# Eight heads' values in one pass: products of 512 columns instead of 256 in a two-layer encoder

## The chip, the cores and the metric

The kernel runs on one core of a Trainium2 chip. The metric is device time in microseconds (us) of one execution, inputs in device memory to output in device memory. TensorE (PE) multiplies matrices into PSUM, which has eight banks of 128 x 512 float32. ACT (ScalarE), DVE (VectorE) and POOL (GpSimd) do the elementwise work, SP (SyncE) issues most transfers.

## The reference, cut to what matters

Two layers over 512 tokens of width 1024; the change is in the first one, neighbourhood attention with 16 heads of 64. Tokens are a grid 64 wide with 8 rows; each query sees a window of all 8 rows and 16 columns, with a learned bias per head.

```python
def mixer_na(xn, w_in, rpb, w_out):
    q, k, v, z = jnp.split(xn @ w_in, 4, axis=-1)      # each (1, 512, 1024)
    o = neighbourhood_attention(q, k, v, rpb)          # 16 heads of 64
    return (o * jax.nn.silu(z)) @ w_out

for i in range(2):
    xn = rmsnorm(x, norm_g[i])
    y = mixer_na(...) if i == 0 else mixer_mla(...)
    h = x + y
    gate = jax.nn.sigmoid(rmsnorm(h, ple_norm[i]) @ ple_w_gate[i])
    x = h + gate * (p[i] @ ple_w_proj[i])
return rmsnorm(x, final_norm)
```

The part of interest is `v = xn @ w_in[:, 2048:3072]`, for all 512 tokens and 16 heads.

## The kernel before, in words

**Precision.** Each operand of a large product is kept as two float32r parts, a high part (a rounded copy, made by ACT) and the rest (made by DVE or POOL). A product then takes three terms: high x high, low x high, high x low. In names, `xh`, `xl` are the two parts of the normalised input turned to columns; `whi`, `wlo` those of a weight.

**Loading weights.** `load_w` (L68) takes 128 x 1024 elements, 512 KB: a transfer from SP into `wraw`, a copy to `whi` on ACT (L78), a subtraction to `wlo` on POOL (L79). Each of the three tiles has three buffers, which all weights of this stage share in turn.

**The first layer's heads.** `na_heads` (L213) goes over eight pairs of heads. `project(j)` makes what pair j needs: for even j first the values of the four heads of pairs j and j+1, then the queries (`sa`, `sb`, 24 products of 512 columns, two copies on ACT, two subtractions on DVE) and the keys (`da`, `db`, `la`, `lb`, likewise, four copies and two subtractions). Values are made token tile by token tile: for each of four tiles `kt` of 128 tokens, 24 products with 128 tokens of `xh` or `xl` held in TensorE and 256 weight columns streamed, over eight k and three terms, the terms one after the other. So every tile wants both loads of its group (`na_v`, 128 x 4 x 256 each) at once. The result goes from bank `mm` to a tile `vt` of 128 x 512, where `v_split` (L204) lays each head's high part and rest side by side (one copy on ACT, L89, one subtraction on DVE, L91). There are eight buffers `vt`, two groups of four heads.

`attend(j)` runs `na_head` (L296) for both heads of the pair: 8 score products of 256 columns (bank `S`, L318 and L319), maximum and exponential on DVE and ACT (L325 to L337), scaling on POOL (L341), 7 transposes of 128 x 128 (bank `T`, L352 and L354), a split on ACT and DVE, and 8 output products with the values held (bank `O`, L366). `combine` adds the halves, `gated` multiplies by the gate where it is ready. Three of the eight gates are made after the last pair (`z_phase`), and the output projection (`out_proj`, L380) follows.

**PSUM.** The eight banks have tags: `mm` two, `S` two, `T` three, `O` one (L63).

**What sets the order.** The code is written as a sequence, `project(j + 1)` ahead of `attend(j)`. The frame it is written in simulates the timeline and plans each engine's order from it, so that instructions of later steps come forward where their operands and buffers are there; the planned order of each engine is then fixed. Buffers of one tag go round in the order in which the code asks for them. A `tile_pool` is memory for a stage; the next stage's tiles lie where the last one's were, and wait tile by tile.

Of the kernel before, what the change touches and what calls it, by code (L numbers as in the profile page):

```python
# [14 lines left out]
F32R = mybir.dt.float32r  # L15
# [4 lines left out]
P = 128  # L20
S = 512
D = 1024
NT = S // P
KD = D // P
# [9 lines left out]
def win(t, r0, r1, off, dims):  # L34

    b = t[r0:r1]
    return bass.AP(tensor=b.tensor, offset=b.offset + off, ap=[list(b.ap[0])] + [list(d) for d in dims])


class Trunk:  # L40
# [99 lines left out]
    def terms(w, xT, ks):  # L140
        whi, wlo = w
        xh, xl = xT
        W = lambda a, k: a[:, k * P:(k + 1) * P]
        X = lambda a, k: a[k // 4][:, k % 4, :]
        t = [(W(whi, k), X(xh, k)) for k in ks]
        t += [(W(whi, k), X(xl, k)) for k in ks]
        t += [(W(wlo, k), X(xh, k)) for k in ks]
        return t
# [64 lines left out]
    def na_heads(self, pool, xT, zs, oT):  # L213
        nc, a = self.nc, self.a
        xh, xl = xT
        X = lambda t, k, kt: t[k // 4][:, k % 4, kt * P:(kt + 1) * P]
        V, A, U = {}, {}, {}

        def project(j):
            if j % 2 == 0:  # L220
                g = j // 2
                wv = [self.load_w(a["na_v"][g, c], 1024) for c in range(2)]
                vts = V[g] = []
                for kt in range(4):
                    ps = self.psum("mm")
                    W = lambda s, k: wv[k // 4][s][:, (k % 4) * 256:(k % 4 + 1) * 256]
                    t = [(X(xh, k, kt), W(0, k)) for k in range(KD)]
                    t += [(X(xl, k, kt), W(0, k)) for k in range(KD)]
                    t += [(X(xh, k, kt), W(1, k)) for k in range(KD)]
                    self.mms(ps[:, :256], t)  # L230
                    vt = pool.tile([P, S], F32R, name="vt", tag="vt", bufs=8)
                    self.v_split(vt, ps[:, :256])
                    vts.append(vt)
            wq = self.load_w(a["na_qk"][j], 1024)
            psq = self.psum("mm")
            self.proj_T(psq, wq, xT)
            sa = pool.tile([P, S], F32R, name="sa", tag="qs", bufs=4)
            sb = pool.tile([P, S], F32R, name="sb", tag="qs", bufs=4)
            nc.scalar.activation(sa[0:64], psq[0:64], AF.Copy, scale=0.125)
            nc.scalar.activation(sb[64:128], psq[64:128], AF.Copy, scale=0.125)  # L240
            nc.vector.scalar_tensor_tensor(sa[64:128], psq[0:64], 0.125, sa[0:64].bitcast(F32),
                                           op0=ALU.mult, op1=ALU.subtract)
            nc.vector.scalar_tensor_tensor(sb[0:64], psq[64:128], 0.125, sb[64:128].bitcast(F32),
                                           op0=ALU.mult, op1=ALU.subtract)
            s0 = []
            for s in (sa, sb):
                e0 = pool.tile([P, P], F32R, name="s0", tag="s0", bufs=4)
                nc.vector.tensor_copy(e0.rearrange("p (a b) -> p a b", a=2),
                                      win(s, 0, P, 0, [[448, 2], [1, 64]]).bitcast(F32))
                s0.append(e0)  # L250
            wk = self.load_w(a["na_qk"][8 + j], 1024)
            psk = self.psum("mm")
            last = self.proj_T(psk, wk, xT)
            da = pool.tile([P, S], F32R, name="da", tag="kd", bufs=4)
            db = pool.tile([P, S], F32R, name="db", tag="kd", bufs=4)
            la, lb = self.rest_k[j % 2]
            nc.scalar.activation(da[0:64], psk[0:64], AF.Copy)
            nc.scalar.activation(da[64:128], psk[0:64], AF.Copy)
            nc.scalar.activation(db[64:128], psk[64:128], AF.Copy)
            nc.scalar.activation(db[0:64], psk[64:128], AF.Copy)  # L260
            nc.vector.tensor_tensor(out=la[0:64], in0=psk[0:64], in1=da[0:64].bitcast(F32), op=ALU.subtract)
            nc.vector.tensor_tensor(out=lb[64:128], in0=psk[64:128], in1=db[64:128].bitcast(F32), op=ALU.subtract)
            A[j] = (sa, sb), s0, (da, db), (la, lb)
            return last

        def attend(j):
            sq, s0, dk, kl = A.pop(j)
            O = []
            for e in range(2):
                c = (2 * j + e) % 4 * P  # L270
                O.append(self.na_head(pool, 2 * j + e, sq[e], s0[e], dk[e], kl[e],
                                      [vt[:, c:c + P] for vt in V[j // 2]]))
            U[j] = self.combine(pool, O[0], O[1], 2 + NLATE)
            if j in zs:
                self.gated(U[j], zs[j], oT, j)


        self.rest_k = []
        for i in range(2):
            la = pool.tile([P, S], F32R, name=f"la{i}", bufs=1)  # L280
            lb = pool.tile([P, S], F32R, name=f"lb{i}", bufs=1)
            nc.gpsimd.memset(la[64:128].bitcast(F32), 0.0)
            nc.gpsimd.memset(lb[0:64].bitcast(F32), 0.0)
            self.rest_k.append((la, lb))
        last = project(0)
        for j in range(8):
            if j < 7:
                last = project(j + 1)
            attend(j)
        late = range(8 - NLATE, 8)  # L290
        zs.update(self.z_phase(a["na_z"], xT, late, self.last_exp.ins))
        for j in late:
            self.gated(U[j], zs[j], oT, j)
        return last.ins
# [594 lines left out]
def layouts(i):  # L889
# [3 lines left out]
    c = np.ascontiguousarray  # L893
    f = {}
# [9 lines left out]
    def tiles(w, n):  # L904
        k, m = w.shape
        return w.reshape(k // P, P, m // n, n).transpose(2, 1, 0, 3)

    w = i["na_w_in"][0]
    f["na_qk"] = c(tiles(w[:, :2048], P).reshape(16, P, 1024))
    f["na_z"] = c(tiles(w[:, 3072:], P).reshape(8, P, 1024))  # L910
    f["na_v"] = c(tiles(w[:, 2048:3072], 256).reshape(4, P, 2, 1024).transpose(0, 2, 1, 3))

    def rows(w):
        return c(tiles(w, S).reshape(2, P, 4, 1024).transpose(0, 2, 1, 3))

    f["na_o"] = rows(i["na_w_out"][0])
    f["mla_o"] = rows(i["mla_w_out"][0])
    f["gate"] = c(np.stack([rows(i["ple_w_gate"][l]) for l in range(2)]))
    f["proj"] = c(np.stack([tiles(i["ple_w_proj"][l], S).reshape(2, P, 1024) for l in range(2)]))
    w = i["mla_w_in"][0]  # L920
# [3 lines left out]
    w = i["mla_w_qb"][0].reshape(384, H, 96)  # L924
# [4 lines left out]
    w = i["mla_w_kvb"][0].reshape(256, H, 128)  # L929
# [49 lines left out]
```

## Time and profile before

| | |
|---|---|
| Three runs, median | 672.58 us (672.41 to 675.2) |
| Profiled execution | 671.05 us, of it span 668.9 us from the first to the last instruction |
| Granted TensorE clock | 0.998 |
| TensorE, busy | 659.1 us, 99% of the span, 3559 products |
| ACT, DVE, POOL, busy | 407.9, 368.4, 394.3 us (61%, 55%, 59%) |
| Loads of the value weights | 8 of 512 KB |
| Value products of this layer | 384 of 128 x 256, starting from 44.7 to 56.9, 80.7 to 97.6, 124.6 to 139.1 and 166.9 to 183.5 us |

A row of the timeline gives the start in us, the length of the row's instructions together, the engine, the line of the code, what is written and read, the shape and the count; in brackets the idle time ahead of it and who ended it. Successive products overlap, so that the price of one is the distance between starts. A row of a window gives the busy time and the count of each engine in a stretch of the span. A row of groups gives a count, the busy time, the mean length in ns, and the idle time ahead.

### The profile page before, as it was taken

To read this page: it belongs to the slowest core of one execution; us is meant where nothing else is said; L and a number is where in the kernel's file an instruction comes from. 1 tells how busy PE (TensorE), PEld (TensorE's weight loads), DVE (VectorE), ACT (ScalarE), POOL (GpSimd) and SP (SyncE) were. 2 spreads that over 40 slices of the span, in tenths; PEclk is the share of its full clock that TensorE was granted. 3 is DMA by queue.
4 is the path that set the end of the run, shared out by engine and by line. 5 is a ranking of instruction groups with operands and counts; after the bars stand their busy time and mean duration, and the time that the engine had idled before them with its cause. 6 is when DMAs were issued, how large, how long until landed. Compare 5 with 4: busy or idle time off the path is not lost.

```text
span 668.9 us, 10166 instructions
## 1 busy us (share of the span) xinstructions
PE 659.1 (99%) x3559; PEld 565.8 (85%) x3559; DVE 368.4 (55%) x828; ACT 407.9 (61%) x813; POOL 394.3 (59%) x322
## 2 busy tenths in 40 slices
PE   9999999999999999999999999999999999999995
PEld 6888898988988888888899887888888888888885
DVE  7461554747746613453624613888888875145434
ACT  7753766657757652653444635887989887436423
POOL 0395546666576565853044526786959786758411
PEclk9999999999999999999999999999999999999999
DMA  9934213222223128534133334120111222664022
GB/s 320 344 121 147 99 53 138 88 86 96 68 99 116 60 98 299 182 110 137 73 116 112 104 102 140 58 75 16 57 49 63 64 97 96 238 247 157 33 79 94
DMA packets 32530, 79.11 MB, mean 118 GB/s; under 512 B 4192, under 2 KB 9056, under 8 KB 32480
## 3 DMA queue, kind: packets, MB, share of 16 engines
q1 hardware_dynamic: 32048, 77.94, 33.9%
q8 instruction: 28, 0.46, 0.3%
q10 hardware_dynamic: 432, 0.52, 0.2%
q14 instruction: 22, 0.18, 0.1%
HBM read 66.92 MB, written 8.39 MB: 113 GB/s over the span
## 4 chain that ended last, share of the span: by engine, by line
PE 92%; POOL 2%; DVE 2%; ACT 1%; DMA 1%; issue 1%; POOLq 0%; SPq 0%; DVEq 0%; ACTq 0%
PE ps_mm L102 50%; PE ps_S L102 12%; PE ps_mm L533 6%; PE ps_T L128 6%; PE ps_O L644 4%; PE ps_T L102 3%; PE ps_O L102 3%; PE ps_O L366 2%; PE ps_mm L173 2%; PE ps_T L354 1%; PE ps_S L319 1%; PE ps_S L318 1%; POOL ex L629 1%; DMA wraw<-proj 1%; DMA qe<-rl 1%
## 5 line engine op out<-in xcount | busy, mean ns | idle before, releaser
L79 POOL TENSOR_TENSOR wlo<-wraw,whi 128x1024 fp32r<-128x1024 f32 (+5 forms) x107 | 209.8, 1978 | 100.3 <-ACT whi L78 79.3
L78 ACT ACTIVATE whi<-wraw 128x1024 fp32r<-128x1024 f32 (+5 forms) x108 | 93.2, 886 | 66.5 <-issue 18.0
L629 POOL TENSOR_TENSOR ex<-ex,rc 128x512 f32<-128x512 f32 x64 | 65.9, 1038 | 25.5 <-DVE rc L628 16.6
L102 PE MATMUL ps_mm<-whi,hnT 128*128 128x512 f32 (+1 forms) x272 | 70.2, 378 | 0.0
L102 PEld LDWEIGHTS ps_mm<-whi,hnT 128*128 128x128 f32 x272 | 49.3, 188 | 9.2
L341 POOL TENSOR_TENSOR ex<-ex,rc 128x128 f32<-128x128 f32 (+1 forms) x64 | 34.3, 560 | 38.0 <-DVE rc L337 36.4
L627 ACT ACTIVATE ex<-ps_S,mx 128x512 f32<-128x512 f32 x64 | 44.0, 688 | 12.3 <-DVE mx L625 11.1
L625 DVE TENSOR_REDUCE mx<-ps_S 128x1 f32<-128x512 f32 x64 | 43.7, 683 | 8.5 <-PE ps_S L102 7.5
L91 DVE TENSOR_TENSOR pt_lo<-ps_T,pt_hi 128x512 fp32r<-128x512 f32 x64 | 43.2, 682 | 7.7 <-ACT pt_hi L89 7.3
L336 ACT ACTIVATE ex<-ex,mx 128x128 f32<-128x128 f32 (+1 forms) x64 | 30.2, 473 | 21.8 <-DVE mx L332 21.4
L102 PE MATMUL ps_mm<-xh,whi 128*128 128x512 f32 x152 | 41.0, 400 | 0.1
L102 PE MATMUL ps_mm<-wlo,hnT 128*128 128x512 f32 (+1 forms) x136 | 40.6, 378 | 0.0
L89 ACT ACTIVATE pt_hi<-ps_T 128x512 fp32r<-128x512 f32 x64 | 37.7, 595 | 4.0 <-PE ps_T L128 3.8
L102 PE MATMUL ps_mm<-xh,wlo 128*128 128x512 f32 x152 | 39.2, 392 | 0.0
L102 PE MATMUL ps_mm<-xl,whi 128*128 128x512 f32 x152 | 38.8, 392 | 0.0
L128 PE MATMUL ps_T<-ident,ex 128*128 128x128 f32 x256 | 38.4, 272 | 0.0
L128 PEld LDWEIGHTS ps_T<-ident,ex 128*128 128x128 f32 x256 | 31.5, 140 | 7.7 <-POOL ex L629 0.4
L194 DVE TENSOR_TENSOR u<-ps_O,u 64x512 f32<-64x512 f32 x32 | 21.9, 686 | 23.1 <-ACT u L193 22.6
L112 POOL TENSOR_TENSOR rs<-ss,half 128x1 f32<-128x1 f32 x20 | 12.7, 638 | 35.0 <-DVE ss L111 34.9
L102 PEld LDWEIGHTS ps_mm<-xl,whi 128*128 128x128 f32 x152 | 28.1, 188 | 5.8
L102 PEld LDWEIGHTS ps_mm<-xh,wlo 128*128 128x128 f32 x152 | 28.1, 188 | 5.5
L463 DVE TENSOR_TENSOR sg<-pe,sg 128x512 f32<-128x512 f32 (+1 forms) x17 | 12.4, 728 | 34.4 <-ACT sg L462 34.4
(342 smaller groups left out, 1668.5 us busy)
## 6 DMA issues: line engine op xcount, KB each, us to landing
pe<-pe SPq DMA_DIRECT2D x32, 256.0 KB, 3.2
wraw<-na_qk SPq DMA_DIRECT2D x16, 512.0 KB, 3.2
wraw<-gate SPq DMA_DIRECT2D x16, 512.0 KB, 3.2
wraw<-na_v SPq DMA_DIRECT2D x8, 512.0 KB, 3.3
wraw<-na_o SPq DMA_DIRECT2D x8, 512.0 KB, 3.4
wraw<-mla_z SPq DMA_DIRECT2D x8, 512.0 KB, 3.5
wraw<-mla_o SPq DMA_DIRECT2D x8, 512.0 KB, 3.3
wraw<-na_z SPq DMA_DIRECT2D x6, 512.0 KB, 5.5
```

The source lines that it names most:

```text
L78: nc.scalar.activation(hi[:, c], raw[:, c], AF.Copy)
L79: f = lambda e, c=c: e.tensor_tensor(out=lo[:, c], in0=raw[:, c], in1=hi[:, c].bitcast(F32), op=ALU.subtract)
L89: self.last_copy = nc.scalar.activation(hi, src, AF.Copy, scale=scale)
L91: nc.vector.tensor_tensor(out=lo, in0=src, in1=hi.bitcast(F32), op=ALU.subtract)
L102: last = self.last_mm = nc.tensor.matmul(out, l, r, start=i == 0, stop=i == n - 1)
L128: self.last_mm = self.nc.tensor.transpose(t[:, i * P:(i + 1) * P], b, self.ident)
L336: self.last_exp = nc.scalar.activation(e, e, AF.Exp, bias=mx[:, qt:qt + 1], accum_out=sm[:, qt:qt + 1])
L341: nc.gpsimd.tensor_tensor(out=e, in0=e, in1=rc[:, qt:qt + 1].to_broadcast([P, e.shape[1]]), op=ALU.mult)
L533: self.last_mm = nc.tensor.matmul(PS[key], *terms[i], start=i == 0, stop=i == len(terms) - 1)
L625: nc.vector.reduce_max(mx, sp, axis=AX.X, negate=True)
L627: nc.scalar.activation(ex, sp, AF.Exp, bias=mx, accum_out=sm)
L629: nc.gpsimd.tensor_tensor(out=ex, in0=ex, in1=rc.to_broadcast([P, S]), op=ALU.mult)
```

## The change

Values are made for eight heads at once (two groups in place of four), in products of 512 columns, chunk by chunk: for each of four loads (`na_v` has the new layout 128 x 2 x 512, two k to a load) all token tiles of the call get their 6 products, so a call keeps one bank open per token tile. The first group is made ahead of everything else, for four token tiles in banks T, T, T and O. The second is made in two bouts of two token tiles each in both banks `mm`, ahead of `attend(1)` and `attend(2)`; each bout loads the whole second group. A finished bank is copied out by two calls of `v_split`, each to a tile `vt` for four heads, as before. There are twelve buffers `vt` instead of eight; the second bout's tiles take the buffers of heads 0 to 3. Values no longer stand in `project`.

```diff
+        def values(g, kts, banks):
+
+            pss = [self.psum(b) for b in banks]
+            for c in range(4):
+                w = self.load_w(a["na_v"][g, c], 1024)
+                for i, (s, r) in enumerate(((0, 0), (1, 0), (0, 1))):
+                    for kt, ps in zip(kts, pss):
+                        for k in (2 * c, 2 * c + 1):
+                            nc.tensor.matmul(ps, X((xh, xl)[s], k, kt), w[r][:, k % 2 * S:(k % 2 + 1) * S],
+                                             start=k == 0 and i == 0, stop=k == KD - 1 and i == 2)
+            for e in range(2):
+                for kt in kts:
+                    V[2 * g + e, kt] = pool.tile([P, S], F32R, name="vt", tag="vt", bufs=12)
+            for kt, ps in zip(kts, pss):
+                for e in range(2):
+                    self.v_split(V[2 * g + e, kt], ps[:, e * 256:(e + 1) * 256])
+
         def project(j):
-            if j % 2 == 0:
-                g = j // 2
-                wv = [self.load_w(a["na_v"][g, c], 1024) for c in range(2)]
-                vts = V[g] = []
-                for kt in range(4):
-                    ps = self.psum("mm")
-                    W = lambda s, k: wv[k // 4][s][:, (k % 4) * 256:(k % 4 + 1) * 256]
-                    t = [(X(xh, k, kt), W(0, k)) for k in range(KD)]
-                    t += [(X(xl, k, kt), W(0, k)) for k in range(KD)]
-                    t += [(X(xh, k, kt), W(1, k)) for k in range(KD)]
-                    self.mms(ps[:, :256], t)
-                    vt = pool.tile([P, S], F32R, name="vt", tag="vt", bufs=8)
-                    self.v_split(vt, ps[:, :256])
-                    vts.append(vt)
             wq = self.load_w(a["na_qk"][j], 1024)
...
-                                      [vt[:, c:c + P] for vt in V[j // 2]]))
+                                      [V[j // 2, kt][:, c:c + P] for kt in range(4)]))
...
+        values(0, range(4), ("T", "T", "T", "O"))
         last = project(0)
         for j in range(8):
             if j < 7:
                 last = project(j + 1)
+            if j in (1, 2):
+                values(1, (2 * j - 2, 2 * j - 1), ("mm", "mm"))
             attend(j)
...
-    f["na_v"] = c(tiles(w[:, 2048:3072], 256).reshape(4, P, 2, 1024).transpose(0, 2, 1, 3))
...
+    f["na_v"] = rows(w[:, 2048:3072])
```

## The prediction

> **What bounds the kernel now.** I read the page first: busy times and the chain that ended last.
>
> ```profile
> span 668.9 us, 10166 instructions
> PE 659.1 (99%) x3559; PEld 565.8 (85%) x3559; DVE 368.4 (55%) x828; ACT 407.9 (61%) x813; POOL 394.3 (59%) x322
> PE 92%; POOL 2%; DVE 2%; ACT 1%; DMA 1%; issue 1%; POOLq 0%; SPq 0%; DVEq 0%; ACTq 0%
> PE ps_mm L102 50%; PE ps_S L102 12%; PE ps_mm L533 6%; PE ps_T L128 6%; PE ps_O L644 4%; PE ps_T L102 3%; PE ps_O L102 3%; PE ps_O L366 2%; PE ps_mm L173 2%; PE ps_T L354 1%; PE ps_S L319 1%; PE ps_S L318 1%; POOL ex L629 1%; DMA wraw<-proj 1%; DMA qe<-rl 1%
> ```
>
> TensorE is busy all the time and makes 92% of the chain; the others stand near 60%. So a product removed counts in full, and work on other engines counts only where TensorE comes to wait. Then the windows, over the stage of the first layer's heads that the change touches:
>
> ```profile
> 45.00:57.00 12.00, 11.48 (x96) 11.28 (x95) 1.90 (x4) 3.17 (x7) 7.18 (x7) 1.00 0.43 138
> 80.00:103.00 23.00, 23.00 (x176) 22.08 (x175) 13.08 (x48) 15.72 (x39) 13.84 (x16) 1.00 0.15 48
> 225.00:243.00 18.00, 17.92 (x102) 15.20 (x101) 9.41 (x24) 12.19 (x24) 10.81 (x11) 1.00 0.09 30
> ```
> ```profile
> 57.00:243.00 186.00, 185.92 (x1131) 165.17 (x1130) 105.92 (x332) 122.79 (x273) 113.90 (x104) 1.00 0.26 88
> ```
>
> Columns: length, then busy time and count of PE, PEld, DVE, ACT, POOL, granted clock (1.00), DMA share, GB/s. From 57 to 243 us TensorE idles 0.08 us of 186; only the first values (45 to 57) lose 0.5. There is almost no idle time to win, so the price of one product decides. It is read from the timeline of TensorE by the distance of starts (the durations overlap):
>
> ```profile
> 46.64 0.64 PE L102 MATMUL ps_mm<-wlo,xh 128*128 128x256 f32 x4
> 47.80 0.74 PE L102 MATMUL ps_mm<-wlo,xh 128*128 128x256 f32 x4 [0.52 <-POOL wlo L79]
> 48.38 1.12 PE L102 MATMUL ps_mm<-whi,xh 128*128 128x256 f32 x8
> ...
> 57.02 2.00 PE L102 MATMUL ps_mm<-xh,whi 128*128 128x512 f32 x8
> ...
> 67.92 1.98 PE L102 MATMUL ps_mm<-xh,whi 128*128 128x512 f32 x8
> ```
>
> **The products.** From 48.38 to 57.02 lie three token tiles of 24 products of 256 columns: 8.64/72 = 0.1200 us each. From 57.02 to 67.92 lie 48 products of 512 columns: 10.90/48 = 0.2271 us. Now the values take 4 groups x 4 tiles x 24 = 384 narrow products, 46.08 us. Afterwards it is 2 x 4 x 24 = 192 wide ones, 43.60 us. The columns are the same; two narrow products cost 12.9 ns more than one wide one. Term 1: -2.48 us.
>
> The Trainium skill, TensorE: Matmul & The Clock Gate, section Back-to-back issue gap, gives a warm distance of N/2.4 + 2.5 ns. By it two narrow products cost only 2.5 ns more than a wide one, term 1 would be an estimated -0.48 us, and the time below would end 2.0 us higher. The rows differ from it (120.0 where it gives 109.2, 227.1 where it gives 215.8), so they decide.
>
> **The wait for the low half.** The first group runs all eight k of the high weights, then wants the low half of the second load. From 46.64, eight products take 48.38 - 46.64 = 1.74 us where 8 x 0.1200 = 0.96 would do: 0.78 us lost. Why it is late:
>
> ```profile
> 42.40 3.00 POOL L796 TENSOR_TENSOR xl<-xT,xh 128x512 fp32r<-128x512 f32 x2
> 45.35 4.75 POOL L79 TENSOR_TENSOR wlo<-wraw,whi 128x1024 fp32r<-128x1024 f32 x2
> ```
> ```profile
> 44.16 1.05 ACT L78 ACTIVATE whi<-wraw 128x1024 fp32r<-128x1024 f32 x1
> ```
>
> POOL is in xl until 45.35; the second low half is ready at 47.7. The new order goes load by load: a load of two k feeds 24 wide products, 5.45 us, and the low half is wanted by the last eight only. If the first wide product starts at 44.7, load 2's low half is wanted at 44.7 + 5.45 + 3.63 = 53.8, 6 us after it is there. The third load takes the slot that the first query weights have now (high half at 44.16, low done at 50.1; wanted at 55.6 and 59.3). The fourth reuses the first load's buffer, free at 50.2: 1.05 + 2.4 us bring it to 53.7, wanted at 61. The two loads put ahead of the queries delay those on SP, but they are wanted only at 66.5. Term 2: -0.78 us, between that and 0.
>
> **Loads and copies.** Each bout loads the whole second group, so 12 loads replace 8. Their prices, and those of the copies:
>
> ```profile
> L78 ACT ACTIVATE whi<-wraw 128x1024 fp32r<-128x1024 f32 x26 | 27.2, 1055 | 23.2 <-issue 17.8 <-PE ps_mm L102 2.4 <-POOL wlo L79 2.0
> L89 ACT ACTIVATE vt<-ps_mm 128x256 fp32r<-128x256 f32 x13 | 4.8, 371 | 1.3 <-PE ps_mm L102 1.3
> ```
> ```profile
> L91 DVE TENSOR_TENSOR vt<-ps_mm,vt 128x256 fp32r<-128x256 f32 x13 | 5.5, 420 | 6.0 <-ACT vt L89 5.7
> ```
> ```profile
> L79 POOL TENSOR_TENSOR wlo<-wraw,whi 128x1024 fp32r<-128x1024 f32 x26 | 62.2, 2397 | 27.5 <-ACT whi L78 15.8 <-PE ps_mm L102 6.0 <-ACT ph L89 2.9
> ```
> ```profile
> wraw<-na_v SPq DMA_DIRECT2D x8, 512.0 KB, 3.3
> ```
>
> ACT gains 4 x 1.055 = 4.2 us, POOL 4 x 2.397 = 9.6 us, SP four issues, the DMA engines 2.1 MB at a share of 0.26. The 16 copies keep their shape. Per pair of heads outside a bout, from the 57 to 243 row: ACT (122.79 - 27.4 - 4.8)/8 + 2 x 1.055 = 13.4 us, DVE (105.92 - 5.5)/8 = 12.6, POOL (113.90 - 62.2)/8 + 2 x 2.397 = 11.3. TensorE's own time for a pair is 48 x 0.2271 = 10.9 plus 46 attention products, at most 0.12 each, 5.5: 16.4 us. A pair with a bout has 27.3 us on TensorE, against ACT 13.4 + 4.2 + 1.5 = 19.1 and POOL 11.3 + 9.6 = 20.9. Inside the bout alone a load feeds 12 products, 2.73 us, where POOL needs 2.40: it holds if POOL does little else then, or attention products stretch the bout. All of it hidden on average; the cover is TensorE's 27 us, and without it up to four low halves would show, 9.6 us.
>
> **The handover of banks.** The bout fills both mm banks at once. Until now four tiles went through them in turn, and the bank of the keys had time to be emptied:
>
> ```profile
> 77.97 1.98 PE L102 MATMUL ps_mm<-xh,wlo 128*128 128x512 f32 x8
> 80.63 0.59 ACT L257 ACTIVATE da<-ps_mm 64x512 fp32r<-64x512 f32 x1
> 80.73 0.89 PE L102 MATMUL ps_mm<-whi,xh 128*128 128x256 f32 x6
> 84.17 0.69 DVE L262 TENSOR_TENSOR lb<-ps_mm,db 64x512 fp32r<-64x512 f32 x1
> 85.33 1.12 PE L102 MATMUL ps_mm<-whi,xh 128*128 128x256 f32 x8
> ```
>
> The keys end at 79.95, their bank is free at 84.86: 4.9 us, bridged by the first value tile and attention products. A bout in written order asks for that bank after two products, 0.45 us. At its end the next queries wait for two copies of the first bank, about 2 x 0.371 + 0.420 = 1.2 us. Two bouts at 4.5 + 1.2 us are 11.4 us if nothing bridges them, 0 if all does. But the planner reorders TensorE by readiness:
>
> ```profile
> 229.48 0.62 PE L102 MATMUL ps_S<-whi,oh 128*128 128x512 f32 x2
> ...
> 242.88 0.61 PE L102 MATMUL ps_mm<-whi,oh 128*128 128x512 f32 x2
> ```
>
> Here the output projection's third tile (bank S) runs 13 us before its first (mm), though the code writes the first one first. With three weight buffers it can run three chunks of the bout's first tile ahead, 18 products or 4.1 us. I stand near the bridged end: one wait like the one shown, 0.52, so term 3: +0.5 us.
>
> **The later pairs.** Values leave the later stretches, so heads 8 to 13 have 16.4 us of TensorE per pair as cover. The fastest pace of before, head 12 to head 14:
>
> ```profile
> 203.23 0.28 PE L318 MATMUL ps_S<-da,s 128*128 128x256 f32 x1
> ...
> 216.26 0.28 PE L318 MATMUL ps_S<-da,s 128*128 128x256 f32 x1
> ```
> ```profile
> 73.53 0.23 PE ps_S L318 x2
> ```
>
> 13.0 us for that pair, under 16.4, though part of it beside less projecting; from head 0 (the last row, of the chain) to head 14 it was 142.7 us, 20.4 a pair, in a stage that had more other work. ACT would be at 13.4/16.4 = 82% there. Bounds: 0, or 2 us for each of four pairs, 8. I take another 0.5 us, near the lower end since pace and loads leave room. Term 4: +0.5. The value buffers: the second bout writes into those of heads 0 to 3, whose readers end a project and a bout earlier; nothing. The output stage's tiles move 8 KB up in memory and may wait for the last reader of the values:
>
> ```profile
> 246.00 1.93 SPq L809 DMA_DIRECT2D r<-x  x4
> ```
>
> It does so already, and chunk 4 of the output projection needs the last heads anyway: nothing, at worst one load's 1.05 + 2.4 = 3.5 us.
>
> **Sum.** -2.48 - 0.78 + 0.5 + 0.5 = -2.26 us. The profiled execution took 671.05 us (span 668.9 and 2.15 around it) and would take 668.8. The median shown is 672.58, 1.5 higher; against it I say 670.3 us, -0.34%. About 0.5%, 3.4 us, is what a measurement here can tell from no change, so this is within it.
>
> **Rivals.** Handover: at the start of each bout TensorE stands, because the planner keeps the written order of the two tiles. Against it the reordering at 229 us; for it that the attention pieces that could fill in are short (8 products, 1 us). At the full 11.4 us the time is 672.58 - 3.26 + 11.4 + 0.5 = 681.2, at half of it 675.5; it turns slower by 0.5% from 6.1 us of standing on.
> Late pairs: heads 8 to 13 can't keep 16.4 us per pair, ACT's queue at 82% being served in order. At 2 us a pair the time is 672.58 - 3.26 + 0.5 + 8 = 677.8; the point is 1.5 us a pair. For it the 20.4 us over the whole stage, against it the 13.0 us pair.
> No narrow-product cost: the 12.9 ns belong to the runs at 48 to 57 us, and wide products in the bouts, alternating between two banks, lose them again. Then 672.58 - 0.78 + 1.0 = 672.8. The page's -0.48 lies near it (672.3), its formula being the rule named above. Against it: both distances hold evenly in neighbouring stretches.
>
> **How the numbers follow.** Forecast 0.50: half of it below 669.2, where nothing is given back (669.3) and the runs' scatter (672.41 to 672.58, the profiled one 671.05) adds; half above. Handover 0.22, of it 0.10 slower. Late pairs 0.16, of it 0.12 slower. No narrow cost 0.12, all within. Faster 0.25, same 0.53, slower 0.22. Range: below, 669.3 less 1 us for scatter, 668.3; above, to 677, just short of the late pairs' 677.8, which leaves out both rivals' upper parts, under 2 in 10 with the low end. The forecast alone: 668.3 to 672.
>
> **What would show it.** Term 1: 192 value products of 128x512 at 0.227 us, none of 128x256 on xh or xl. Term 2: no TensorE wait for wlo in the values' first 22 us. Term 3: TensorE's idle time in the two bouts, under 1 us; waits on DVE lb or vt copies would speak for the handover. Term 4: starts of even heads' first score products 16 to 17 us apart with TensorE full. I am wrong if TensorE idles over 2 us between 45 and 245, or if a wide value product costs over 0.235 us.

## The result, and the profile after

The changed kernel takes 680.53 us (median of 4 runs, 679.05 to 680.75), the kernel before 672.5 (671.36 to 675.2): ratio 1.0117, 95% interval 1.0097 to 1.0137. I had said 670.3 us and a range up to 677. The page of the changed kernel, its span, TensorE and the chain:

```profile
span 678.2 us, 9812 instructions
PE 662.2 (98%) x3367; PEld 558.7 (82%) x3367; DVE 366.2 (54%) x828; ACT 410.7 (61%) x817; POOL 404.8 (60%) x326
PE 92%; DVE 2%; DMA 1%; POOL 1%; ACT 1%; issue 1%; POOLq 0%; SPq 0%; DVEq 0%; ACTq 0%
```

192 products fewer, as intended, and the busy time is higher. The timeline of the first group, first and last rows, shows the two gains:

```profile
46.66 1.52 PE L227 MATMUL ps_T<-whi,xh 128*128 128x512 f32 x6
...
67.97 0.62 PE L227 MATMUL ps_O<-wlo,xh 128*128 128x512 f32 x2
68.42 1.75 PE L102 MATMUL ps_mm<-xh,whi 128*128 128x512 f32 x7
```

96 wide products in 68.42 - 46.66 = 21.76 us are 0.2267 each, with no wait for a low half. The waits of TensorE from 40 to 260 us (engine and line, whom it waited for, total us, times, longest):

```profile
PE ps_mm L102 <- DVE vt L91: 3.9, 1, 3.9
PE ps_S L324 <- DVE mx L334: 1.3, 1, 1.3
PE ps_S L102 <- DVE mx L334: 0.6, 1, 0.6
PE ps_O L372 <- DVE u L194: 0.3, 1, 0.3
```

Together they are 6.1 us, where the prediction named 2 as its sign of being wrong. The first is the copying of the values. It lies behind the second bout; TensorE's timeline there:

```profile
151.33 1.09 PE L227 MATMUL ps_mm<-wlo,xh 128*128 128x512 f32 x4
152.25 0.27 PE L358 MATMUL ps_T<-ident,ex 128*128 128x128 f32 x1
...
154.41 0.28 PE L372 MATMUL ps_O<-pl,vt 128*128 128x256 f32 x1
158.62 3.75 PE L102 MATMUL ps_mm<-xh,whi 128*128 128x512 f32 x8 [3.93 <-DVE vt L91]
162.17 2.96 PE L102 MATMUL ps_mm<-xl,whi 128*128 128x512 f32 x8
164.97 0.39 PE L102 MATMUL ps_mm<-xh,wlo 128*128 128x512 f32 x1
```

The bout's last rows are x4: both tiles end together, so both banks become free late. Attention products fill 2.3 us (152.25 to 154.41 and the last one's 0.12), then TensorE stands for 4.1. Behind that, eight products take 162.17 - 158.62 = 3.55 us, 0.44 each instead of 0.227. The windows say why (the columns as in the prediction; the clock follows the counts):

```profile
150.00:154.50 4.50, 4.50 (x32) 3.92 (x31) 2.71 (x9) 3.52 (x6) 4.50 (x4) 1.00 0.30 93
154.50:158.60 4.10, 0.19 (x2) 0.01 (x1) 4.06 (x11) 3.13 (x10) 4.09 (x4) 0.85 0.53 173
158.60:164.30 5.70, 5.68 (x14) 4.47 (x15) 1.99 (x5) 1.21 (x5) 2.43 (x3) 0.51 0.46 170
164.30:170.00 5.70, 5.70 (x29) 4.77 (x28) 1.73 (x3) 2.76 (x4) 3.12 (x2) 1.00 0.00 0
```
```profile
154.50:157.30 2.80, 0.19 (x2) 0.00 (x0) 2.76 (x8) 1.88 (x7) 2.80 (x2) 1.00 0.38 148
157.50:158.60 1.10, 0.00 (x0) 0.01 (x1) 1.10 (x4) 1.08 (x3) 1.09 (x3) 0.50 0.91 256
```

The granted clock is 0.51 for 5.7 us. The first sixteen products behind the wait take 164.97 - 158.62 = 6.35 us, where 16 x 0.227 = 3.63 would do: another 2.7 us lost. The Trainium skill, TensorE: Matmul & The Clock Gate, Part 1, gives a TensorE that idles through a window of some 3.4 us half its clock until it has been busy for at least as long again. The rows agree with the halving and with the way back, after more than 5 us of work; but the clock was still full up to 157.30 and halved from 157.50 on, so it fell 2.8 to 3.0 us into the idle time, short of that window.

Why were the copies late? DVE and POOL at the same place:

```profile
153.93 1.46 DVE L338 TENSOR_SCALAR mx<-mx 128x2 f32<-128x2 f32 x1
155.30 0.41 DVE L91 TENSOR_TENSOR vt<-ps_mm,vt 128x256 fp32r<-128x256 f32 x1
...
156.52 1.17 DVE L338 TENSOR_SCALAR mx<-mx 128x2 f32<-128x2 f32 x1
157.60 0.55 DVE L91 TENSOR_TENSOR pl<-ps_T,ph 128x384 fp32r<-128x384 f32 x1
158.07 0.74 DVE L91 TENSOR_TENSOR vt<-ps_mm,vt 128x256 fp32r<-128x256 f32 x2
```
```profile
150.63 7.03 POOL L79 TENSOR_TENSOR wlo<-wraw,whi 128x1024 fp32r<-128x1024 f32 x3
```

The negation of two maxima (128x2) takes 1.46 and 1.17 us. Its usual time is 0.17. Of the three low halves on POOL, 2.35 us each, the second ends at 155.36 and the third at 157.66; each negation ends with one of them (155.39 and 157.69). The copies stand behind them in DVE's queue, and on ACT a copy stands behind exponentials that want those maxima:

```profile
153.19 0.38 ACT L89 ACTIVATE vt<-ps_mm 128x256 fp32r<-128x256 f32 x1
155.42 0.40 ACT L342 ACTIVATE ex<-ex,mx 128x128 f32<-128x128 f32 x1 [1.85 <-DVE mx L338]
...
156.69 0.64 ACT L89 ACTIVATE vt<-ps_mm 128x256 fp32r<-128x256 f32 x2
```

To compare kernels I use the length of the stage, from the first value product to the last product that reads the first layer's `xh`. Executions reach its start sooner or later: the profiled ones at 44.73 us before and 46.66 after, but also at 46.66 in a run of the kernel before with one DVE instruction exchanged, so the late start need not come from the change. It follows a slower beginning of TensorE (15 products between 7.5 and 10.5 us in the profile of before, 8 in that of the change); why is not settled. The length leaves that out, and is the better measure than a median, which carries up to 1.9 us of it. It is 242.65 - 44.73 = 197.92 us before and 251.14 - 46.66 = 204.48 after, 6.6 us more. The sum: -2.5 for the products, -0.8 for the low half, +4.1 idle and +2.7 at half clock behind the second bout, +1.5 around the wait for scores at 121 us, +1.2 around the last two waits of the list at 236: +6.2.

### The profile page after: what moved, and what is told of

It reads as the page before. It is cut to its first block, busy times and chain, and to the rows that moved or that the text cites. A ratio compares the mean times of both kernels' runs of the same rounds, so it can differ in the third digit from the quotient of the medians.

```text
span 678.2 us, 9812 instructions
## 1 busy us (share of the span) xinstructions
PE 662.2 (98%) x3367; PEld 558.7 (82%) x3367; DVE 366.2 (54%) x828; ACT 410.7 (61%) x817; POOL 404.8 (60%) x326
## 4 chain that ended last, share of the span: by engine, by line
PE 92%; DVE 2%; DMA 1%; POOL 1%; ACT 1%; issue 1%; POOLq 0%; SPq 0%; DVEq 0%; ACTq 0%
PE ps_mm L102 44%; PE ps_S L102 13%; PE ps_mm L539 6%; PE ps_T L128 6%; PE ps_O L650 4%; PE ps_T L102 3%; PE ps_O L102 2%; PE ps_T L227 2%; PE ps_mm L227 2%; PE ps_O L372 2%; PE ps_mm L173 2%; PE ps_T L360 1%; PE ps_S L324 1%; PE ps_S L325 1%; PE ps_O L227 1%
## 5 line engine op out<-in xcount | busy, mean ns | idle before, releaser
L79 POOL TENSOR_TENSOR wlo<-wraw,whi 128x1024 fp32r<-128x1024 f32 (+5 forms) x111 | 220.6, 2003 | 108.4 <-ACT whi L78 79.1
L78 ACT ACTIVATE whi<-wraw 128x1024 fp32r<-128x1024 f32 (+5 forms) x112 | 97.5, 893 | 79.2 <-issue 18.2
L102 PE MATMUL ps_mm<-xh,whi 128*128 128x512 f32 x152 | 43.1, 414 | 3.9 <-DVE vt L91 3.9
L102 PE MATMUL ps_mm<-xl,whi 128*128 128x512 f32 x152 | 40.7, 401 | 0.0
L102 PEld LDWEIGHTS ps_mm<-xh,whi 128*128 128x128 f32 x152 | 28.1, 196 | 9.0 <-issue 4.1
```

The source lines that it names most:

```text
L78: nc.scalar.activation(hi[:, c], raw[:, c], AF.Copy)
L79: f = lambda e, c=c: e.tensor_tensor(out=lo[:, c], in0=raw[:, c], in1=hi[:, c].bitcast(F32), op=ALU.subtract)
L102: last = self.last_mm = nc.tensor.matmul(out, l, r, start=i == 0, stop=i == n - 1)
```

## Experiments

Theory A: the loss is the handover of both mm banks at the end of the bouts. Theory L, within it: DVE standing behind POOL is what makes the copies late. Rivals: wide products or the early first group do harm by themselves (B); the four additional loads or the memory do (C). A ratio is against runs of the kernel before made beside it, whose median was 672.07 us for the first four experiments and 671.85 for the last three. The change itself was not run again there, so that differences to it go by the stage.

**Only the first group wide.** Heads 8 to 15 are made by the former code, in groups of four, with the former layout of their weights.

```diff
         def project(j):
+            if j in (4, 6):
...
-            if j in (1, 2):
-                values(1, (2 * j - 2, 2 * j - 1), ("mm", "mm"))
```

> Only the first part of the change: heads 0 to 7 wide and ahead of all, heads 8 to 15 as before in products of 256 columns, tile by tile, ahead of the queries of pairs 4 and 6; eight value buffers, eight loads. Theory A, the loss comes from the handover of both mm banks at the end of the second bout: no bout, no loss; 96 pairs of narrow products become wide, -1.24 us, the wait for the low half goes, -0.78: about 670.5 us. Rival B, wide products or the early first group harm the stage by themselves (attention begins 10 us later): 674 or more.

670.97 us, ratio 0.9979 (0.9966 to 0.9993); stage 195.84 us, 2.08 under the kernel before where the two terms give 2.02. The list of TensorE's waits between 40 and 260 us is empty. B falls: wide products pay what the rows of before said, and the later start of attention costs nothing that shows here.

**Bouts in mm and T.** One edit on the changed kernel:

```diff
-                values(1, (2 * j - 2, 2 * j - 1), ("mm", "mm"))
+                values(1, (2 * j - 2, 2 * j - 1), ("mm", "T"))
```

> The changed kernel with one edit: the bouts use one bank mm and one bank T in place of both mm, so that the next queries find an mm bank free. Theory A: the 4.1 us in which TensorE stands after the second bout and the 2.7 us lost to the halved clock behind it are gone, 680.5 - 6.8 = 673.7. Rival C, the four additional loads or the memory of twelve value buffers are to blame: stays within 1 us of 680.5. Another wait may come up on T, where transposes have one bank less.

669.35 us, ratio 0.9962 (0.9951 to 0.9974), stage 195.90 us: 8.6 under the change, 2.0 under before. The loads and the twelve buffers are the same, so C falls. TensorE's timeline around the end of the second bout of this kernel:

```profile
142.84 0.62 PE L227 MATMUL ps_T<-wlo,xh 128*128 128x512 f32 x2
143.30 0.28 PE L324 MATMUL ps_S<-da,sa 128*128 128x256 f32 x1
...
144.01 2.00 PE L102 MATMUL ps_mm<-xh,whi 128*128 128x512 f32 x8
145.85 1.98 PE L102 MATMUL ps_mm<-xl,whi 128*128 128x512 f32 x8
```

The queries follow the bout after 0.7 us, the time of six score products, at the full clock (8 in 1.84 us). Its one wait between 40 and 260:

```profile
PE ps_O L372 <- DVE u L194: 0.4, 1, 0.4
```

The copies are no quicker than in the change. Two negations right behind the bout take 2.50 us together, and the last copy ends at 150.16, 6.9 us after the bout:

```profile
145.82 2.50 DVE L338 TENSOR_SCALAR mx<-mx 128x2 f32<-128x2 f32 x2
...
149.74 0.42 DVE L91 TENSOR_TENSOR vt<-ps_T,vt 128x256 fp32r<-128x256 f32 x1
```

TensorE does not wait for them, because the next queries had a bank. The edit also changes the planned order, from about 106 us on, so this run alone does not separate the bank from the order.

**Another negation on the changed kernel.** A reduction over one element does the same sum without the form that waits.

```diff
-            nc.vector.tensor_scalar(mx[:, hs], mx[:, hs], -1.0, None, op0=ALU.mult)
+            nc.vector.reduce_max(mx[:, hs], mx[:, hs].rearrange("p (a b) -> p a b", b=1), axis=AX.X, negate=True)
```

> The changed kernel with one edit: the maxima are negated by a reduction over one element on DVE in place of a multiplication by -1 (TENSOR_SCALAR, 128x2). In the profile each such multiplication that starts while POOL works ends when POOL's instruction does. Theory L, the copies of the second bout are late because DVE stands in two of them (1.46 and 1.17 us) behind POOL's low halves: about 2.6 us less idle, under the length that halves the clock, 680.5 - 2.6 - 2.7 = 675. Theory A without L (the queue of copies alone): within 1 us of 680.5. The reduction should take 0.1 to 0.2 us whatever POOL does.

672.5 us, ratio 1.0004 (0.9989 to 1.002), stage 197.68 us, 6.8 under the change. The instruction itself in both kernels, the change first (count, then ns least, median, most):

```profile
L338 DVE TENSOR_SCALAR mx<-mx x32: 156/170/2143, 88.7 to 239.5; 128x2 f32<-128x2 f32 x32
```
```profile
L338 DVE TENSOR_REDUCE mx<-mx x32: 138/150/156, 88.8 to 232.6; 128x2 f32<-128x2 f32 x32
```

And the same three low halves, bout and queries in the new trace:

```profile
150.09 7.09 POOL L79 TENSOR_TENSOR wlo<-wraw,whi 128x1024 fp32r<-128x1024 f32 x3
...
154.19 0.28 PE L372 MATMUL ps_O<-pl,vt 128*128 128x256 f32 x1
...
155.69 2.08 PE L102 MATMUL ps_mm<-xh,whi 128*128 128x512 f32 x8 [1.23 <-DVE vt L91]
```
```profile
156.00:162.00 6.00, 6.00 (x30) 5.04 (x29) 1.89 (x4) 3.80 (x9) 5.18 (x7) 1.00 0.58 197
```

Apart from the exchanged form, both traces have the same instructions in the same order on TensorE, ACT, DVE and POOL, from first to last. POOL works as long, and the wait is 1.2 us instead of 3.9; with so short a wait the clock stays at 1.00. So L holds: of the 6.8 us, 2.7 of waiting and 2.7 of clock behind the second bout hang on DVE standing behind POOL, and the waits at 236 (1.2) are gone as well. What is left of the handover is 155.69 - 152.26 = 3.4 us from the bout's end to the queries, in place of 6.4, with 1.2 of it idle. I had expected 5.3; the median fell by 8.0, more than the stage, and its rest is about the size of the earlier or later start (the profiled execution, which starts at 46.67, took 674.11 us). The Trainium skill, SBUF — State Buffer, section Who interferes with whom, says that DVE in a two-port mode, which a tensor_scalar can enter, and POOL exclude each other for the whole instruction, and that a tensor_reduce never contends on trn2. Both rows agree: up to 2.14 us for the one, at most 0.156 for the other. In which mode the multiplication ran, no row tells.

**The same negation on the kernel before.**

> The kernel before with the same other negation alone. TensorE has no idle time in the stage, so both theories say 672.5 within 1 us, while DVE loses about 10 us of busy time (32 x (0.49 - 0.16)). A gain of more than 2 us would mean that the profile of before hides DVE waits that I do not see.

671.24 us, ratio 0.9997 (0.9985 to 1.0009): no difference to be told, as expected. There the same standing still is hidden: no wait on DVE is in TensorE's list. That attention products and the four value tiles bridge it is my explanation and was not tested.

**Both edits.** Bouts in mm and T, and the reduction.

> Both edits on the changed kernel: bouts in banks mm and T, maxima negated by a reduction. If the two act on the same loss (theory A with L: the reduction only shortens the handover that T takes away), it is within 1 us of the 669.35 of bouts in mm and T alone. If DVE's standing behind POOL costs TensorE elsewhere too, it is 1 to 2 us better, 668.

669.56 us, ratio 0.9959 (0.9945 to 0.9974), stage 195.20. The time cannot be told from that of bouts in mm and T alone, and the planned order is the same in both: with a bank free for the queries, the negations behind POOL, up to 2.4 us each, make a difference of 0.7 us between the two stages. The two edits act on the same loss.

**The wait filled.** Fourteen products that nobody reads, behind the second bout.

```diff
...
+            if j == 2:
+                ps = self.psum("T")
+                with self.tc.issue_after(self.last_v.ins):
+                    for i in range(14):
+                        nc.tensor.matmul(ps, X(xh, 0, 0), xh[0][:, 0, :], start=True, stop=True)
```

> The changed kernel with 14 additional products of 512 columns into a bank T that nobody reads, behind the last product of the second bout; they add 14 x 0.227 = 3.2 us of work that the result doesn't need. The wait after the bout was 4.1 us and the clock was at half for the 5.7 us behind it. Theory A: the additional work fills the wait, the next queries begin when they did, and the clock stays: 680.5 - 2.7 = 677.8 in spite of the additional work. If the products at 0.427 us were not from the idle time: 680.5 to 683.7.

674.73 us, ratio 1.0039 (1.0026 to 1.0052), stage 199.96 us: 4.5 us less than the change with 3.2 us more work. I had expected 2.7. (`self.last_v` is the bout's last product.) Its timeline:

```profile
146.66 1.07 PE L227 MATMUL ps_mm<-wlo,xh 128*128 128x512 f32 x4
147.57 3.34 PE L299 MATMUL ps_T<-xh 128*128 128x512 f32 x14
...
151.43 2.09 PE L102 MATMUL ps_mm<-xh,whi 128*128 128x512 f32 x8
```

The queries begin 151.43 - 147.57 = 3.9 us after the bout; in the change it was 158.62 - 152.25 = 6.4. The granted clock stays at 1.00. But the plan differs (attention's output products now come behind the queries), so this does not separate the clock from the wait: it shows that with the gap filled the half clock stays away, not what the clock alone costs.

**Only the second bout in mm and T.**

> The changed kernel with only the second bout in mm and T, the first in both mm banks as in the change. Theory A by the waits seen in the trace: the second bout's 6.8 us go, the first's 1.5 us (a score product behind DVE at 121 us) stay: 673.7 to 674. If the first bout's wait is worth nothing by the end: 672. If the whole plan only happened to fall badly: no relation to either sum.

670.64 us, ratio 0.998 (0.9967 to 0.9993), stage 196.68: 7.8 under the change where the second bout's waits gave 6.8. The first bout's wait stays and is the only one in the list:

```profile
122.72 0.36 PE L324 MATMUL ps_S<-db,s 128*128 128x256 f32 x1 [1.33 <-DVE mx L334]
```

Against bouts in mm and T throughout it is 0.8 us longer in the stage, about the difference of their waits (1.3 here, 0.4 there). The additional 1.0 us has about the size of the waits at 236, which are gone here as well. The median is 3 us below what I had expected, of which the stage explains 1. The other 2 lie outside it. The start probably makes most of them: the profiled execution, which reaches the stage at 46.77 as late as that of the change, took 672.15, 1.5 above the median.

In this kernel the planned order differs from the change's from about 136 us on, and in that with both bouts in mm and T from 106. Two different orders, both with a bank left for the queries, lose nothing behind the second bout; that speaks for the bank and against an order that fell badly by chance.

## Why the prediction was wrong

**The products** (term 1): right. 0.2267 us against 0.2271 forecast; the 2.5 ns a pair by the formula of the Trainium skill (TensorE: Matmul & The Clock Gate, Back-to-back issue gap) do not hold here: in the first experiment half of the products and the low half brought 2.08 us, where 0.24 + 0.78 would have been 1.0.

**The low half** (term 2): right; no such wait in the first group.

**Loads and copies**: the 9.6 us on POOL were counted as hidden behind TensorE's 27 us per pair. They do not delay TensorE by being late themselves, as I had feared: no row shows TensorE waiting for `wlo`. Low halves delay DVE, whose negations end when POOL's instruction ends. Those in question are not even the additional ones: by the order in which weights are loaded and split, the three from 150.63 on are of the query and key weights that come next, and the bout's own last one ran before them. I had compared busy times engine by engine and missed that two of them hold each other up. The row was there, in the groups of DVE from 57 to 243 us of the kernel before (busy us, mean ns), and beside it the same line's least, median and most:

```profile
L332 DVE TENSOR_SCALAR mx<-mx 128x2 f32<-128x2 f32 x32 | 15.2, 490 | 0.4
```
```profile
L332 DVE TENSOR_SCALAR mx<-mx x32: 152/170/2093, 77.5 to 232.0; 128x2 f32<-128x2 f32 x32
```

A mean three times the median tells of a wait inside the instruction.

**The handover of banks** (term 3): this is the step that failed. I expected the stop at the bout's start, 4.5 us, and little at its end, 1.2 us from the copies' own lengths, and took 0.5 for both bouts. The start went as I argued: the planner ran one tile ahead of the other, and no wait shows. The end of the second bout took 6.4 us from the bout's last product to the next queries, 2.3 of them filled, because the copies stood in line behind other work on ACT and DVE; their own length did not set it. Of the 6.4, 2.9 are DVE standing behind POOL, as the exchanged negation shows. Once idle for 4.1 us, TensorE lost 2.7 more by its clock, a cost that had no place in my sum. At the first bout's end another 1.5 went. With the negation exchanged the second bout's end still takes 3.4 us, nearly three times the 1.2 that I had worked out; that 1.2 of it are idle is a chance likeness. There the copies still follow, among others, a weight's high half of 1.06 us and two exponentials on ACT. The rival named the right place with the wrong end; that its full 11.4 us would have given 681.2, near the 680.5 measured, is luck.

**The later pairs** (term 4): about right. In the kernel with bouts in mm and T the stage is 2.0 us under before, where terms 1 and 2 alone give 3.3: 1.3 us given back, 0.4 of it as a wait that the profile names, against the 0.5 taken; the other 0.9 is not settled. Pairs do keep pace: in that kernel the first score products of heads 6, 8, 10 and 12 start at 156.74, 173.03, 189.35 and 205.65 us, 16.3 apart where I had 16.4.

## What to carry to other kernels

When a change closes several PSUM banks at the same moment, ask not how long the copies take but what stands in the queues of the copying engines ahead of them, and keep one bank of the next consumer's tag out of it: moving one of two banks to another tag turned a loss of 6.6 us in the stage into a gain of 2.0. When the first engine is at 99%, a wait is dearer than its length if it is long enough to halve the clock. And busy shares of DVE and POOL may not be added up as if independent: look for small DVE instructions whose longest time is ten times their median.

## What the runs showed of the hardware

A DVE multiplication of 128x2 elements took 0.156 to 2.143 us in the same kernel. Those that began 0.13 us or more ahead of the end of POOL's running instruction ended 20 to 32 ns after that end; those that began within its last 0.06 us took 0.16 us. A reduction of the same elements took 0.138 to 0.156 in the same places of the same order. After 4.1 us of idle time eight TensorE products took 0.44 us each instead of 0.227, at a granted clock of 0.51 over 5.7 us; after an idle time of 1.4 us (154.19 to 155.69 less the last product's 0.1) they did not. In the one long wait the clock fell 2.8 to 3.0 us into the idle time.
